# SwiGLU on one core: storing four rows per partition at once from a shared slot

## The chip, the cores and the metric

The kernel runs on 1 core of one Trainium2 chip. The metric is device time in microseconds, the median of several executions. All data is float32.

## The reference

The input `x` has 8,192 rows of 8,192 columns. Each row is split into a left half `a` and a right half `b`, and the output row (4,096 columns) is `a` times SiLU of `b`.

```python
a, b = np.split(x, 2, axis=-1)
silu_b = b / (1 + np.exp(-b))
return a * silu_b
```

So 268.44 MB are read and 134.22 MB are written, and each element is used once.

## The kernel before

A tile holds one or two neighbouring rows per partition, on 128 partitions. A row of `x` is 32 KiB, a row of the output 16 KiB. `rows` (line 26) lists the 33 tiles: one row per partition in the first and the last tile, two in the 31 between them. A two-row tile is 8.39 MB when it is loaded, and 4.19 MB when it is stored. Each partition's part is one contiguous piece of DRAM, in `x` (64 KiB) and in the output (32 KiB).

There are three SBUF slots of 64 KiB per partition, used in turn (`BUFS`, line 24). Tile i uses slot i modulo 3 for everything: `load` (line 50) fills it from the SP queue, `swiglu` (line 57) has ScalarE replace the right half by its SiLU ("gate") and VectorE multiply the halves ("product"), and the product is written over the front of the same slot; `store` (line 73) writes it out. A slot's next load waits for its store. The order is written by hand: three loads, and then for each tile the gates, the products, the store, and the load of the tile three further on. `follows_from_others` (line 40) drops those waits that follow from others, so that each instruction waits only for what comes last.

The first and the last tile are computed in two column halves (`by_halves`, line 69), tiles 1 and 31 row by row, all others in one gate (line 62) and one product (line 64).

All loads are issued by SP (line 51). Stores (line 77) are issued by ScalarE, except that the last three come from SP and two in the middle (tiles 17 and 19) from GpSimd. Each issuing engine has a DMA queue of its own, and all queues are served by the same 16 DMA engines: in the profile, q1 is SP's, q10 ScalarE's and q0 GpSimd's.

Of the kernel before, what the change touches and what calls it, by code (L numbers as in the profile page):

```python
# [1 line left out]

# [4 lines left out]

_SILU = mybir.ActivationFunctionType.Silu


@with_exitstack
def kernel(
    ctx: ExitStack,
    tc: tile.TileContext,
    x: bass.AP,
    out: bass.AP,
):

    nc = tc.nc  # L20
    N, M = x.shape
    half = M // 2
    P = nc.NUM_PARTITIONS
    BUFS = 3

    rows = [1] + [2] * (N // P // 2 - 1) + [1]
    first = [sum(rows[:i]) * P for i in range(len(rows))]
    last = len(rows) - 1

    pool = ctx.enter_context(tc.tile_pool(name="sbuf", bufs=1))  # L30
    ctx.enter_context(tc.manual_schedule())
    slots = [pool.tile([P, 2 * M], x.dtype, name=f"slot{s}") for s in range(BUFS)]
    loads, gates, prods, stores = ([[] for _ in rows] for _ in range(4))
    newest = {}

    def in_dram(t, i, width):

        return bass.AP(t.tensor, first[i] * width, [[rows[i] * width, P], [1, rows[i] * width]])

    def follows_from_others(inst, i, current, earlier):  # L40


        targets = [t for kind in current for t in kind[i]]
        targets += [t for kind in earlier for j in range(i % BUFS, i, BUFS) for t in kind[j]]
        for t in targets:
            if t is not newest.get(inst.ins.engine):
                tc.declare_no_dep(inst.ins, t.ins, reason="ordered by the other waits")
        newest[inst.ins.engine] = inst

    def load(i):  # L50
        inst = nc.sync.dma_start(  # L51
            out=slots[i % BUFS][:, : rows[i] * M], in_=in_dram(x, i, M)
        )
        follows_from_others(inst, i, [], [loads, gates, prods])
        loads[i].append(inst)

    def swiglu(i, k0, k1, c0=0, cw=half):
        view = slots[i % BUFS].rearrange("p (k s c) -> p k s c", k=2, s=2)
        a = view[:, k0:k1, 0, c0 : c0 + cw]
        b = view[:, k0:k1, 1, c0 : c0 + cw]  # L60
        o = slots[i % BUFS][:, : 2 * half].rearrange("p (k c) -> p k c", k=2)
        gate = nc.scalar.activation(out=b, in_=b, func=_SILU)  # L62
        follows_from_others(gate, i, [], [loads, gates, prods, stores])
        prod = nc.vector.tensor_mul(out=o[:, k0:k1, c0 : c0 + cw], in0=a, in1=b)  # L64
        follows_from_others(prod, i, [loads], [loads, gates, prods, stores])
        gates[i].append(gate)
        prods[i].append(prod)

    def by_halves(i):
        for c0 in range(0, half, half // 2):  # L70
            swiglu(i, 0, 1, c0, half // 2)

    def store(i):
        eng = nc.scalar if i < last - 2 else nc.sync
        if i % 2 and last // 2 <= i < last // 2 + 4:
            eng = nc.gpsimd
        inst = eng.dma_start(  # L77
            out=in_dram(out, i, half), in_=slots[i % BUFS][:, : rows[i] * half]
        )
        follows_from_others(inst, i, [loads, gates], [loads, gates, prods, stores])  # L80
        stores[i].append(inst)

    for i in range(BUFS):
        load(i)
    for i in range(last):
        if i == 0:
            by_halves(i)
        elif i in (1, last - 1):
            swiglu(i, 0, 1)
            swiglu(i, 1, 2)  # L90
        else:
            swiglu(i, 0, rows[i])
        store(i)
        if i + BUFS <= last:
            load(i + BUFS)
    by_halves(last)
    store(last)


# [1 line left out]
_INS = ['x']  # L101
_OUTS = [((8192, 4096), 'float32')]


# [23 lines left out]
```

## Time and profile before

| | |
|---|---|
| median of 3 runs | 935.07 us (934.86 to 935.34) |
| span of the profiled execution | 933.2 us |
| DMA, mean over the span | 432 GB/s, 402.67 MB |
| VectorE busy | 278.7 us (30%), 37 instructions |
| ScalarE busy | 226.8 us (24%), 38 instructions |
| product of two rows / one row / half a row | 8.69 / 4.43 / 2.29 us |
| gate of two rows / one row / half a row | 7.03 / 3.61 / 1.90 us |
| load of 8.39 MB, from issue to landing (median) | 37.7 us |
| store of 4.19 MB on ScalarE's queue, the same | 33.5 us |
| store of 4.19 MB on GpSimd's queue, the same | 34.4 us |

The profile gives the span from the first to the last instruction of one execution; it has no time of its own for that execution beyond the span, and the median of the runs is 1.87 us above it. An engine's busy time leaves out the issuing of DMAs. The time from a DMA's issue to its landing includes the time that it shares with, or waits behind, other DMAs on the same 16 engines. The trace also has a record of every DMA packet, with its size, its queue, its start and its length.

### The profile page before, as it was taken

The page shows a single profiled execution, that of the slowest core. Times are in us where ns is not written, and L with a number is a line of the kernel's source. Part 1 is how long each engine was busy: PE and PEld are TensorE (multiplying, and loading weights), DVE is VectorE, ACT ScalarE, POOL GpSimd, SP SyncE. Part 2 cuts the span into 40 slices and gives each one's busy share as a digit, 9 for nine tenths or more (in the row PEclk, how much of TensorE's full clock was granted, in tenths as well). Part 3 has the DMA queues.
Part 4 walks back from the last instruction along what each step waited for, and adds up shares of the span by engine and source line. Part 5 has one row for each costly group of instructions (what it writes and reads, how often), then busy time and mean ns, then how long its engine had stood idle before and what let it go on. Part 6 is the DMA issues. An engine that isn't in the chain of part 4 may idle for free.

```text
span 933.2 us, 220 instructions
## 1 busy us (share of the span) xinstructions
DVE 278.7 (30%) x37; ACT 226.8 (24%) x38; POOL 1.4 (0%) x6
## 2 busy tenths in 40 slices
DVE  1312333123331233312333113332133321333242
ACT  2331133311333203332033320233202332023330
POOL 0000000000000000000000000000000000000000
DMA  9999999999999999999999999999999999999998
GB/s 405 405 449 431 423 451 444 409 444 433 444 427 434 442 410 448 428 433 442 434 421 441 445 417 444 428 454 427 420 457 405 449 427 428 448 445 409 427 444 388
DMA packets 9505, 402.67 MB, mean 432 GB/s; under 512 B 1056, under 2 KB 1056, under 8 KB 1056
## 3 DMA queue, kind: packets, MB, share of 16 engines
q1 hardware_dynamic: 5184, 278.92, 69.1%
q10 hardware_dynamic: 4032, 115.35, 28.6%
q0 software_dynamic: 288, 8.39, 2.1%
q14 instruction: 1, 0.01, 0.0%
HBM read 268.44 MB, written 134.22 MB: 431 GB/s over the span
## 4 chain that ended last, share of the span: by engine, by line
DMA 72%; DVE 11%; ACT 8%; issue 6%; another core or an unknown queue 1%; DVEq 0%; POOL 0%; SPq 0%; ACTq 0%; POOLq 0%
DMA slot<-in_x_dram 40%; DMA out_dram<-slot 32%; DVE slot L64 11%; ACT slot L62 8%; DVEq L123 0%; POOL out_dram L77 0%; SPq L51 0%; ACTq L77 0%; DVEq L64 0%; POOLq L123 0%
## 5 line engine op out<-in xcount | busy, mean ns | idle before, releaser
L64 DVE TENSOR_TENSOR slot<-slot 128x8192 f32<-128x8192 f32 (+2 forms) x37 | 278.7, 7539 | 636.7 <-ACT slot L62 636.5
L62 ACT ACTIVATE slot<-slot 128x8192 f32<-128x8192 f32 (+2 forms) x37 | 225.6, 6107 | 684.3 <-DMA slot<-in_x_dram 684.3
L77 POOL DMA_DIRECT2D out_dram<-slot x2 | 1.2, 600 | 568.9 <-DVE slot L64 568.9
L62 ACT ACT_TABLE_LOAD x1 | 1.3, 1283 | 0.7 <-PEq L112 0.7
L112 POOL MEMSET const-bfloat16-1.0<- 128x1 bf16 x1 | 0.1, 102 | 0.0
L112 POOL MEMSET const-float32-0.0<- 128x1 f32 x1 | 0.1, 99 | 0.2 <-issue 0.2
L112 POOL MEMSET const-float32-1.0<- 128x1 f32 x1 | 0.1, 99 | 0.0
L112 POOL MEMSET const-uint8-127<- 128x1 uint8 x1 | 0.1, 99 | 0.0
## 6 DMA issues: line engine op xcount, KB each, us to landing
out_dram<-slot ACTq DMA_DIRECT2D x27, 4096.0 KB, 33.5
slot<-in_x_dram SPq DMA_DIRECT2D x2, 4096.0 KB, 13.6
out_dram<-slot POOLq DMA_DIRECT2D x2, 4096.0 KB, 34.4
out_dram<-slot SPq DMA_DIRECT2D x2, 4096.0 KB, 20.4
out_dram<-slot ACTq DMA_DIRECT2D x1, 2048.0 KB, 28.1
out_dram<-slot SPq DMA_DIRECT2D x1, 2048.0 KB, 16.8
slot<-in_x_dram SPq DMA_DIRECT2D x31, 37.7
```

The costliest lines, as they stand in the source:

```text
L62: gate = nc.scalar.activation(out=b, in_=b, func=_SILU)
L64: prod = nc.vector.tensor_mul(out=o[:, k0:k1, c0 : c0 + cw], in0=a, in1=b)
L77: inst = eng.dma_start(out=in_dram(out, i, half), in_=slots[i % BUFS][:, : rows[i] * half])
L112: nc = _bacc.Bacc("TRN2", target_bir_lowering=False, num_devices=1)
```

## The change

The three slots get different roles. Slot 0 is now a side slot, slots 1 and 2 are main slots. The two-row tiles are replaced: after a one-row tile (side slot) and a two-row tile (first main slot), which are stored as before, come 15 groups of four neighbouring rows per partition, and then a one-row tile. That is again 64 rows per partition.

A group is loaded in two DMAs of two rows per partition each: the first pair into a main slot, the second pair into the side slot. From one partition to the next the address in `x` now moves by four rows (128 KiB), while each piece is 64 KiB. The first pair's product goes to the front half of the main slot, in one gate and one product. The second pair is computed row by row from the side slot, and its products go to the back half of the main slot. The group is then stored in one DMA of 64 KiB per partition, 8.39 MB.

The side slot is free for the next group's second pair as soon as the group's last product is done, without a store. A main slot is loaded again after its group's store. The main slots alternate from group to group.

All loads are issued by SP, in this order: the next group's first pair (waits for the store of the group before this one), then the next group's second pair (waits for this group's last product). Stores are issued by ScalarE, those of groups 7, 8 and 9 by GpSimd, and that of group 14 and of the last row by SP. There are 33 loads as before, and 18 stores instead of 33. Waits are now named for each instruction (`after`, which drops all others).

```diff
-    BUFS = 3
-    rows = [1] + [2] * (N // P // 2 - 1) + [1]
...
+    PITCH = 4
+    groups = (N // P - 4) // 4
...
+    slots = [pool.tile([P, 2 * M], x.dtype, name=f"slot{s}") for s in range(3)]
+    side, mains = slots[0], slots[1:]
...
+    def swiglu(src, row, rows, dst, at, *needed, pieces=1):
+        view = src.rearrange("p (k s c) -> p k s c", k=2, s=2)
+        packed = dst.rearrange("p (k c) -> p k c", k=4)
+        last = None
+        for c0 in range(0, half, half // pieces):
+            cols = slice(c0, c0 + half // pieces)
+            a = view[:, row : row + rows, 0, cols]
+            b = view[:, row : row + rows, 1, cols]
+            gate = after(nc.scalar.activation(out=b, in_=b, func=_SILU), *needed)
+            last = after(
+                nc.vector.tensor_mul(out=packed[:, at : at + rows, cols], in0=a, in1=b), gate
+            )
+        return last
+
+    first = load(side, 0, 1, 1)
+    second = load(mains[0], P, 2, 2)
+    lead = [load(mains[1], 3 * P, PITCH, 2)]
+    base = 3 * P
+    firsts = {0: lead[0]}
+
+    done = swiglu(side, 0, 1, side, 0, first, pieces=2)
+    stored = store(nc.scalar, side, 0, 1, 1, done)
+    free_side = stored
+
+    def group(g):
+        return base + 4 * (g if PITCH != 4 else g * P)
+
+    seconds = {0: load(side, group(0) + 2, PITCH, 2, free_side)}
+    swiglu(mains[0], 0, 1, mains[0], 0, second)
+    done = swiglu(mains[0], 1, 1, mains[0], 1, second)
+    free = {0: store(nc.scalar, mains[0], P, 2, 2, done), 1: None}
+    last = None
+    for g in range(groups):
+        m = (g + 1) % 2
+        other = 1 - m
+        if g + 1 < groups:
+            firsts[g + 1] = load(mains[other], group(g + 1), PITCH, 2, free[other])
+        else:
+            last = load(mains[other], N - P, 1, 1, free[other])
+        swiglu(mains[m], 0, 2, mains[m], 0, firsts[g])
+        for k in range(2):
+            done = swiglu(side, k, 1, mains[m], 2 + k, seconds[g])
+        eng = nc.scalar if g + 1 < groups else nc.sync
+        if groups // 2 <= g < groups // 2 + 3:
             eng = nc.gpsimd
...
+        free[m] = store(eng, mains[m], group(g), PITCH, 4, done)
+        if g + 1 < groups:
+            seconds[g + 1] = load(side, group(g + 1) + 2, PITCH, 2, done)
+    done = swiglu(mains[1 - m], 0, 1, mains[1 - m], 0, last, pieces=2)
+    store(nc.sync, mains[1 - m], N - P, 1, 1, done)
```

In `load` and `store` the arguments after the slot are the first row, the step in rows from one partition to the next, the number of rows per partition, and what the DMA waits for.

More of the change, by code (lines that the diff above doesn't have):

```diff
@@ L23 @@
     P = nc.NUM_PARTITIONS
-    BUFS = 3
-    rows = [1] + [2] * (N // P // 2 - 1) + [1]
-    first = [sum(rows[:i]) * P for i in range(len(rows))]
-    last = len(rows) - 1
+    PITCH = 4
+    groups = (N // P - 4) // 4
     pool = ctx.enter_context(tc.tile_pool(name="sbuf", bufs=1))
     ctx.enter_context(tc.manual_schedule())
-    slots = [pool.tile([P, 2 * M], x.dtype, name=f"slot{s}") for s in range(BUFS)]
-    loads, gates, prods, stores = ([[] for _ in rows] for _ in range(4))
+    slots = [pool.tile([P, 2 * M], x.dtype, name=f"slot{s}") for s in range(3)]
@@ L34, with after @@
+    side, mains = slots[0], slots[1:]
     newest = {}
[L36 to L46, printed above, removed]
+    def after(inst, *needed):
+        for t in (t for ts in everything for t in ts):
+            if t not in needed and t is not inst and t is not newest.get(inst.ins.engine):
@@ L47, in follows_from_others, with in_dram, load @@
                 tc.declare_no_dep(inst.ins, t.ins, reason="ordered by the other waits")
         newest[inst.ins.engine] = inst
-    def load(i):
+        history.append(inst)
+        return inst
+    def in_dram(t, start, step, rows, width):
+        return bass.AP(t.tensor, start * width, [[step * width, P], [1, rows * width]])
+    history = []
+    everything = [history]
+    def load(slot, start, step, rows, *needed):
         inst = nc.sync.dma_start(
-            out=slots[i % BUFS][:, : rows[i] * M], in_=in_dram(x, i, M)
+            out=slot[:, : rows * M], in_=in_dram(x, start, step, rows, M)
@@ L53, in load @@
         )
[L54 to L75, printed above, removed]
-            eng = nc.gpsimd
[L77 to L97, printed above, removed]
+        return after(inst, *needed)
+    def store(eng, slot, start, step, rows, *needed):
+        inst = eng.dma_start(
+            out=in_dram(out, start, step, rows, half), in_=slot[:, : rows * half]
+        )
+        return after(inst, *needed)
@@ new lines, in swiglu @@
+    def swiglu(src, row, rows, dst, at, *needed, pieces=1):
[9 more added lines that the diff above has]
+                nc.vector.tensor_mul(out=packed[:, at : at + rows, cols], in0=a, in1=b), gate
+            )
+        return last
```

## The prediction

> **What bounds the kernel now.** I read the page's slices and queue table first, then windows over single stretches, then the chain of waits, then groups by form. The page shows compute engines that are mostly idle and DMA engines that are not:
>
> ```profile
> DVE 278.7 (30%) x37; ACT 226.8 (24%) x38; POOL 1.4 (0%) x6
> ...
> DMA  9999999999999999999999999999999999999998
> ...
> q1 hardware_dynamic: 5184, 278.92, 69.1%
> q10 hardware_dynamic: 4032, 115.35, 28.6%
> q0 software_dynamic: 288, 8.39, 2.1%
> ```
>
> The three queues' shares add up to 99.8% of 16 engines' span. Windows (length, busy of DVE, ACT, POOL, clock, DMA share, GB/s) say whether the mix of traffic changes the rate:
>
> ```profile
> 3.62:21.70 18.08, 4.49 (x2) 3.71 (x2) 0.00 (x0) 1.00 1.00 433
> ...
> 118.00:466.00 348.00, 104.31 (x12) 84.37 (x12) 0.00 (x0) 1.00 1.00 434
> 898.00:930.00 32.00, 13.26 (x4) 10.84 (x4) 0.00 (x0) 1.00 0.99 427
> ```
>
> The first stretch is loads alone, the second loads and stores mixed, the third stores with the one compute drain. All run at 427 to 434 GB/s. The trace's packet records give the reason: each DMA engine moves one packet after another, one of 65,536 bytes every 2.414 us, one of 32,768 bytes every 1.209 us, a completion word in 0.006 us, in every stage. A load (8.39 MB) is 8 packets per engine, 19.3 us; a store of before is 8 half packets, 9.7 us; together 8 x (2.414 + 1.209) + 0.012 = 29.00 us, and the chain's period is 29.0 us (three of its steps are 87.0). So there is no hole in the steady part. The bound is bytes, and the span can change in three ways only: the packets' sum, a hole in the queues, or the two ends. The chain shows the compute time that will matter, at a slot done as two single rows (start, length, what):
>
> ```profile
> 35.47 3.62 ACT slot L62
> ...
> 39.12 4.44 DVE slot L64
> ...
> 43.65 4.44 DVE slot L64
> 48.09 0.02 issue
> 48.11 0.34 ACTq L77
> ```
>
> The load landed at 35.44 and the store was issued at 48.11, 12.67 us later: one gate, two products, the second gate hidden behind the first product. Today another slot's load and a store fill the DMA engines meanwhile.
>
> **The change, part by part.** Names: f(g) is the load of a group's first pair into a main slot, c(g) that of the second pair into the side slot, S(g) the group's store, T the moment at which the group's last product ends.
>
> Removed and merged: 30 stores of two rows become 15 of four, in 64 KiB packets. Per engine 15 x 8 times two half packets (2.418 us) become one packet (2.414 us), 0.48 us, and 15 completion words at 0.006 go, 0.09 us. Sum -0.6 us. Loads keep number, bytes and packets.
>
> Compute: 15 two-row pairs keep their form; the other 15 become 30 + 30 single-row instructions (gate 3.61, product 4.43 us). That adds about 0.17 us of DVE per pair, hidden: f(g+1) has landed by about T + 15 and needs 15.8 us, and c(g+1) lands only at T + 45.
>
> Steady part: a group moves 25.17 MB, 58.0 us at 434 GB/s, exactly two periods of now, if the queues never run dry. c(g) ends in the engines; T comes 0.4 (from last packet to landing, by load 0) + 12.7 = 13.1 us later. Meanwhile only f(g+1) is queued, 19.3 us of it, so 6.2 us are left at T. At T S(g) is issued on ScalarE and c(g+1) on SP. The records show queues taking turns packet by packet, so the store now has half of the engines while it runs (a third before): 8 of its packets and 7 of loads, 15 x 2.414 = 36.2 us from its first packet. That first packet came 5.0 to 5.3 us after issue for the first store of the trace and 3.5 to 6.2 us for the second, both into a queue of loads alone. S(g) therefore lands 40.1 to 42.8 us after T, SP issues f(g+2) at once, and its packets start 1.0 to 1.6 us later (the first load: issue 0.74, first packets 1.74 to 2.30), at 41.1 to 44.4. The load queue runs dry at 6.2 + 19.3 + 19.3 = 44.8. The margin is 0.4 to 3.7 us, thin but positive: I take 0 here.
>
> What waits newly queue: SP's f(g+2) waits behind c(g+1), which was issued 40 us earlier; ScalarE is held by S(g)'s wait for 4.4 us behind the second gate, and what stands behind it, the gate of f(g+1), has no data until about 15 us after T. Both cost nothing.
>
> GpSimd stores: three in a row of 8.39 MB instead of two of 4.19 MB. The group of their issues has 600 ns each, and theirs took 34.4 us to land against 33.5. Started 0.3 us late and 0.9 us slower, their margin is -0.8 to 2.5 us, and a gap is bounded by one packet, 2.4 us, in up to two of three groups. I take 0 and keep +4.8 for the range.
>
> The end: this is where it pays. Before, at the last products (898 to 918) the queue still held two stores, and the last window is full. Afterwards the final one-row load (4.19 MB, 9.66 us) is all that is queued behind c(14). From c(14)'s last packet to S(14)'s first: 0.4 + 12.7 + 1.0 to 1.6 = 14.1 to 14.7 us. Covered by the load: 9.66. Hole on all 16 engines: 4.4 to 5.0 us, I take 4.8 because SP's wait and a spread of engines come on top of the low end. It doesn't depend on when the last load starts, since a late start would only move the hole ahead of it. Behind the hole, S(14) (19.3 us) hides the last row's gates and products (some 4.6 us after T), so the last store follows without a second hole.
>
> The start: three loads of the same packets, and the two early stores as before. c(0) waits for the first store as its predecessor did (47.5), f(1) for the second (81.1), while c(0) lasts until about 86. Cost 0.
>
> Sum: -0.6 + 4.8 = +4.2 us. The profiled span of 933.2 becomes 937.4; the median of the runs lies 1.87 us above that span (what lies around it), so 939.3 us. Bounds of these terms: 3.7 to 4.5, that is 938.8 to 939.6, and to 944.1 with the GpSimd gaps.
>
> A doubt is the loads' step from one partition to the next, now 128 KiB where it was 64 KiB. The trace has steps of 32 KiB (first load) and 64 KiB (the rest) at the same time per byte, 1.213 and 2.418 us a packet, so I take 0; the far end is the most stretched load packet near the start, 3.05 us instead of 2.42, which over 30 x 8 packets would be 150 us. The Trainium skill, DMA: Bandwidth & Descriptors, section Latency and other measured facts, speaks against the change here: copies fell from 214 to 207 GB/s per direction at a row pitch of 512 KiB and lower at 2 MiB, and it has no value for 128 KiB. If that first loss held here already, an estimate from that page is 3.4% of 580 us of load packets, 20 us, 959 in all.
>
> **The rivals.**
> 1. The margin fails (for: 0.4 us at its thin end, and landing waits for the slowest of 16 engines; against: both stores seen lie inside it). Every time S(g) slips by one packet, f(g+2) arrives some 2 us after the queue ran dry; the hole lengthens what is left at the next T, so every second group pays: 7 x 2 = 14 us, 953. 8%.
> 2. Only the GpSimd stage slips: 1 or 2 gaps of 2.4 us, 941.7 to 944.1. 8%.
> 3. The 128 KiB step slows load packets (for: new in this kernel; against: 32 to 64 KiB cost nothing). Each 1% on 240 packets of 2.418 us per engine costs 5.8 us; the time for 1% is 945, and nothing in the rows bounds it short of the 150 us above. 4%.
> 4. The descriptors don't go out whole: if 64 KiB stores were cut into two packets of 32 KiB, S(g) would keep a third of the engines, land after c(g+1) has ended, and leave about 1.6 us dry in each of 14 groups, 22 us: 962. Against: loads already go as 65,536-byte packets, 3,968 of them. 2%.
> 5. Not slower: a store has a cost beside its packets, and 15 fewer give it back along the steady part. It offsets the end's hole to within 0.2% from (4.2 - 1.9) / 15 = 0.15 us per store, and turns it to a gain of over 0.2% from 0.41. For: load packets near the first stores last 0.2 to 0.6 us longer. Against: 29.00 us of packets in a period of 29.0 leave under 0.05. At 0.15 to 0.4 it gives 933.3 to 937; beyond, at most 402.65 MB / 434 GB/s = 927.8 plus the ends. 6%, 2 of it on the faster side. The same page's section Anatomy of one DMA has a fixed 2.0 us per DMA; if that were exposed, 15 stores less would be worth 30 us, about 909, and the row's 434 GB/s excludes it.
>
> **How the numbers follow.** The forecast has the remaining 72%, with 938.5 to 940.5 as its own range. The range for 8 in 10 adds the GpSimd stage: 937.8 to 944.2; outside lie rivals 1, 4, 5 and most of 3, some 19%. About 0.2%, 1.9 us, is what a measurement of this kernel can tell from no change: 933.2 to 936.9 is the same. Faster 2%, same 4% (the rest of rival 5), slower 94%.
>
> **What would show it.** Right: packets of 65,536 bytes at 2.418 us on the store queue; period 58.0 us in the chain; DMA share 1.00 in windows from 100 to 890; a window near 905 to 915 with a share of about 0.5, from the last load's end to S(14)'s first packet; f(g+2) issued 1 to 4 us before c(g+1) ends. Wrong: a share under 1.00 every 116 us (rival 1), only from 530 to 720 (2), load packets over 2.418 us (3), 32,768-byte packets on the store queue (4), or no hole before the last large store.

## The result, and the profile after

The changed kernel takes 972.99 us (median of 4 runs, 970.25 to 975.44) against 935.21 us of the kernel before (4 runs, 934.86 to 936.44): a ratio of 1.0399, 95% interval 1.0386 to 1.0413. The forecast was slower, 939.3 us in a range of 937.8 to 944.2. The direction was right; the loss is 37.8 us, nine times the 4.1 us forecast. The profiled execution took 972.03 us with a span of 970.2 us, so the span grew by 37.0 us.

The page of the changed kernel, the same rows as before:

```profile
DVE 279.6 (29%) x51; ACT 228.1 (24%) x52; POOL 1.9 (0%) x7
...
DMA  9999999999999999999999999999799999999979
...
q1 hardware_dynamic: 5040, 278.92, 68.9%
q10 hardware_dynamic: 1872, 98.57, 23.5%
q0 software_dynamic: 432, 25.17, 6.0%
```

Compute is as before. The DMA row has two dents, one at about 690 us and one near the end. The queues' shares add up to 98.4%, so idle engines explain less than half of a loss of 4%. Windows of the changed kernel (length, busy of DVE, ACT and POOL, clock, DMA share, GB/s) show the rest:

```profile
207.00:218.00 11.00, 8.73 (x2) 5.74 (x2) 0.00 (x0) 1.00 0.92 399
218.00:224.00 6.00, 0.03 (x1) 0.00 (x0) 0.00 (x0) 1.00 1.05 371
224.00:262.00 38.00, 8.69 (x1) 7.03 (x1) 0.00 (x0) 1.00 1.00 433
...
408.00:466.00 58.00, 17.45 (x3) 14.15 (x3) 0.00 (x0) 1.00 0.99 414
...
684.00:690.00 6.00, 0.00 (x0) 0.51 (x1) 0.00 (x0) 1.00 0.05 22
...
940.00:945.00 5.00, 3.96 (x2) 2.22 (x2) 0.00 (x0) 1.00 0.54 229
```

Read the DMA share and the rate side by side. In one whole group (408 to 466) the engines are busy for 0.99 of the time and move 414 GB/s, not 434. From 218 to 224, right after the group's store and the next side load were issued at 218.06, the share is full and the rate is 371 GB/s: the packets themselves last longer. (Windows this short carry an error of a packet, which is why a share can exceed 1.) From 224 to 262, while the store runs, the rate is 433 GB/s. Two windows are real holes: 684 to 690, and 940 to 945 near the end.

The packet records put numbers on it. "Stretch" below is the time of packets beyond 2.418 us (64 KiB) and 1.213 us (32 KiB), summed and divided by 16 engines; "idle" is the time without a packet, per engine, from 3 us on. A "main load" fills a main slot (f in the prediction), a "side load" the side slot (c).

| us per engine | before | after | difference |
|---|---|---|---|
| stretch | 0.8 | 24.7 | +23.9 |
| idle | 0.4 | 14.2 | +13.7 |
| fewer packets and completion words (forecast's term) | | | -0.6 |
| sum | | | +37.0 |

The sum is the span's growth. The idle time is 6.0 us near 690, 4.4 us in the hole between the last load and the last large store, and 3.8 us in small pieces. The stretch sits almost wholly on load packets: of the 4,096 packets of 64 KiB on SP's queue (128 of them are the last large store's) 575 lasted over 30 ns too long, the worst 4.55 us, against 9 of the 1,792 on the two other store queues.

The chain of waits is now made of side loads and single-row compute, with a period that is not 58.0:

```profile
397.53 0.02 issue
397.54 46.89 DMA slot<-in_x_dram
444.43 0.02 issue
444.45 3.62 ACT slot L71
448.08 0.02 issue
448.10 8.77 DVE slot L73 x2
456.87 0.02 issue
456.89 49.12 DMA slot<-in_x_dram
```

From the issue of one side load (397.54) to that of the next (456.89) are 59.35 us. From landing (444.43) to issue are 12.46 us, as the prediction had it.

### The profile page after: what moved, and what is told of

It reads as the page before. It is cut to its first block, busy times and chain, and to the rows that moved or that the text cites. A ratio compares the mean times of both kernels' runs of the same rounds, so it can differ in the third digit from the quotient of the medians.

```text
span 970.2 us, 238 instructions
## 1 busy us (share of the span) xinstructions
DVE 279.6 (29%) x51; ACT 228.1 (24%) x52; POOL 1.9 (0%) x7
## 4 chain that ended last, share of the span: by engine, by line
DMA 78%; DVE 13%; ACT 6%; DVEq 0%; issue 0%
DMA slot<-in_x_dram 71%; DVE slot L73 13%; DMA out_dram<-slot 8%; ACT slot L71 6%; DVEq L138 0%
## 5 line engine op out<-in xcount | busy, mean ns | idle before, releaser
L73 DVE TENSOR_TENSOR slot<-slot 128x4096 f32<-128x4096 f32 (+2 forms) x51 | 279.6, 5511 | 669.6 <-ACT slot L71 669.5
L71 ACT ACTIVATE slot<-slot 128x4096 f32<-128x4096 f32 (+2 forms) x51 | 226.8, 4480 | 717.7 <-DMA slot<-in_x_dram 717.7
```

What stands on the lines that cost most here:

```text
L71: gate = after(nc.scalar.activation(out=b, in_=b, func=_SILU), *needed)
L73: nc.vector.tensor_mul(out=packed[:, at : at + rows, cols], in0=a, in1=b), gate
```

## The experiments

Three theories are tested below. A: loads step 128 KiB from partition to partition and collide in memory. B: loads that run alone on all 16 engines are slow at any step (in the changed kernel no store runs for about a third of each group's time). R: what counts is how late a main load is issued, by what is still queued ahead of it.

### The step of the loads (A)

Each of these three changes the third argument of the groups' loads, and the first row where needed:

```diff
-firsts[g + 1] = load(mains[other], group(g + 1), PITCH, 2, free[other])
+firsts[g + 1] = load(mains[other], group(g + 1), 2, 2, free[other])        # e1; e2: 5, e3: 8
-seconds[g + 1] = load(side, group(g + 1) + 2, PITCH, 2, done)
+seconds[g + 1] = load(side, group(g + 1) + 256, 2, 2, done)                # e1; e2: + 2, 5; e3: + 2, 8
```

> The changed kernel with the loads of the 15 groups stepping two rows (64 KiB) from one partition to the next, as in the kernel before, instead of four: a group's two loads take its first 256 rows and its second 256. Stores, waits, order and sizes stay, so the products land in other rows of the group than they belong to; the run is for its time. Theory A (the 128 KiB step makes load packets collide in memory): 64 KiB load packets fall from a mean of 2,510 to about 2,420 ns, 23 us go, 947 to 950 us, with the two holes left (6 and 5 us). Theory B (loads that run alone on all 16 engines are slower at any step): packets stay near 2,510 ns, 970 to 975 us.

> The same with a step of five rows (160 KiB), so that a group's loads read other rows than they should; the run is for its time. Theory A in the form 'a step of 128 KiB repeats over the memory's channels': an odd multiple of 32 KiB spreads again, 947 to 950 us. Theory A in the form 'any step above the piece's own 64 KiB, that is a gap between pieces, costs': 970 us or more. Theory B: 970 to 975 us.

> The same with a step of eight rows (256 KiB), rows read are not those that belong to the output; the run is for its time. Repeating channels: twice the step is worse than 128 KiB, at least 60 us of stretch instead of 24, 1,005 us or more. Theory B: 970 to 975 us. Gaps between pieces: about as with 128 KiB or somewhat more, 970 to 985 us.

The fourth gives the kernel before the 128 KiB step:

```diff
+        if rows[i] == 1 or i == 31:
+            return bass.AP(t.tensor, first[i] * width, [[rows[i] * width, P], [1, rows[i] * width]])
+        start = P + (i - 1) // 2 * 4 * P + (i - 1) % 2 * 2
+        return bass.AP(t.tensor, start * width, [[4 * width, P], [1, 2 * width]])
```

> The kernel before with its two-row tiles 1 to 30 taken in pairs from blocks of four rows per partition: loads step 128 KiB, stores 64 KiB with 32 KiB pieces. All else as before, and the output too. If the step alone slows load packets: 30 x 8 packets stretched by 92 ns each, about 22 us, 955 to 960 us. If it needs stretches in which loads run alone on all 16 engines, which this kernel hardly has: 935 to 938 us.

| run | step of loads | time, us | ratio to before | stretch, us per engine |
|---|---|---|---|---|
| changed kernel | 128 KiB | 972.99 | 1.0399 [1.0386, 1.0413] | 24.7 |
| e1 | 64 KiB | 975.78 | 1.0427 [1.034, 1.0514] | 23.9 |
| e2 | 160 KiB | 970.83 | 1.0374 [1.0337, 1.0411] | 23.7 |
| e3 | 256 KiB | 976.19 | 1.0432 [1.035, 1.0513] | 28.2 |
| e4, kernel before | 128 KiB | 935.03 | 0.9994 [0.9983, 1.0005] | 0.8 |

e1 to e3 have two runs each, and e3's profile is of its longer one (979.27 us).

Theory A falls in both directions: taking the step back to 64 KiB brings nothing, and giving it to the kernel before costs nothing. In that kernel the rate stays what it was:

```profile
118.00:466.00 348.00, 104.30 (x12) 84.35 (x12) 0.00 (x0) 1.00 1.00 434
```

### How late a load is issued (R), and the stores beside it

e5 leaves out the second side row's compute, so that everything behind the side load comes 4.4 us earlier:

```diff
-        for k in range(2):
-            done = swiglu(side, k, 1, mains[m], 2 + k, seconds[g])
+        done = swiglu(side, 0, 1, mains[m], 2, seconds[g])
```

> The changed kernel without gate and product of the second row of each side pair; its part of the output is stored as it stands. DMAs and their order stay. The last product comes 4.4 us earlier after the second load's landing, so that the next main load is issued some 7 to 9 us, not 2.8 to 4, before the load queue runs dry. Theory R (a load packet lasts longer when a load's descriptors come to a load queue that is about to run dry, and when the next DMAs come to such a queue): the stretch falls from 24 us per engine to under 4, the hole behind the GpSimd store (6 us) goes, the hole at the end falls from 4.9 to about 0.5: 936 to 942 us. Theory B (loads alone on all engines are slow; stores still fill only 38.6 of 58 us): stretch stays over 20 us, 957 to 966 us. Theory S (a 64 KiB store that comes to a queue empty of stores stretches the load packet before it): the 1.3 us at each store's issue stay, about 17 us, 951 to 957 us.

952.04 us (948.67 to 955.41), ratio 1.0182 [1.0097, 1.0267]. Stretch fell from 24.7 to 10.5 us, the hole near 690 is gone, idle is 4.4 us. The time lies in the range of S, but the stretch is neither the 4 us that R expected nor the 17 to 20 of S and B. It was not spread evenly, and that is what the run taught. Windows of e5:

```profile
100.00:420.00 320.00, 71.31 (x11) 60.26 (x11) 0.00 (x0) 1.00 1.01 435
440.00:690.00 250.00, 56.89 (x9) 45.71 (x9) 1.73 (x3) 1.00 1.00 420
```

Five groups run at full rate, with stores that still fill only two thirds of the time; then five are slow. What separates them is the load time still queued when the main load was issued (the mean of the 16 engines): 3.9 us and more in the first five, 1.9 to 3.1 in the others. Theory B can't give the first window, and S (every 64 KiB store that comes to a queue without stores costs 1.3 us) can't either. R was right in kind, and its boundary lies near 3 us.

e6 cuts each group's store in two; the output is whole:

```diff
...
+        pair = swiglu(mains[m], 0, 2, mains[m], 0, firsts[g])
+        early = store(eng, mains[m], group(g), PITCH, 2, pair)
         for k in range(2):
             done = swiglu(side, k, 1, mains[m], 2 + k, seconds[g])
-        free[m] = store(eng, mains[m], group(g), PITCH, 4, done)
+        late = store(eng, mains[m][:, 2 * half :], group(g) + 2, PITCH, 2, done)
+        free[m] = [early, late]
```

> The changed kernel with each group's store cut into two DMAs: the main pair's rows as soon as their product is done, the side pair's rows at the group's end (32 KiB pieces, 64 KiB step). The main slot is loaded again when both have landed. The late store lands some 33 us after its issue instead of 43, and a store is nearly always queued. Theories R, B and S all expect the stretch to go (under 3 us), and the end's hole to be filled by the early store: 934 to 938 us. If it stays over 15 us, none of them holds.

935.77 us (8 runs), ratio 1.0000 [0.9982, 1.0018]. Stretch 1.0, idle 0.8 us, and the window is that of the kernel before:

```profile
118.00:466.00 348.00, 104.71 (x18) 84.91 (x18) 0.00 (x0) 1.00 1.00 434
```

So the slots' new roles, the side slot and the row-by-row compute cost nothing that the runs show. The whole loss hangs on storing the group in one piece at its end. Two things changed together here: a store nearly always runs, and the main loads also come earlier, with 4.1 us of loads or more left. The next runs take them apart.

e7 and e8 make the loads of the kernel before late, by repeating a product that doesn't change the result:

```diff
+        if cw == half and k1 - k0 == 2:
+            for w in (half,):                    # e8: (half, half // 2)
+                prod = nc.vector.tensor_mul(
+                    out=o[:, 1:2, :w], in0=view[:, 1:2, 0, :w], in1=view[:, 1:2, 1, :w]
+                )
...
```

> The kernel before, with the second row's product of every whole tile made once more (4.4 us of VectorE; the output is the same). Store and next load of a slot come 4.4 us later, so a load is issued about 4 us, not 8.5, before the load queue runs dry. Stores stay 32 KiB pieces, and a store is always queued. Theory R: load packets stretch here too, some 10 to 40 us, 945 us or more. Theories B and S: nothing, 935 to 937 us (the end may take 2 us more).

> The same with 6.7 us more of VectorE for each tile: a load is issued about 1.8 us before the load queue runs dry, and comes 0.5 us or less before it does. Theory R: more stretch than in the run with 4.4 us, 955 us or more. Theories B and S: 935 to 941 us, with short holes at most.

e7: 938.93 us (938.08 to 940.88), ratio 1.0036 [1.002, 1.0052]. 28 loads, from 84 to 869 us, were issued with 0.1 to 2.4 us of loads left, later than most in the changed kernel, and none cost more than 0.05 us of stretch: beside each, packets of a store were running or began within 2.0 us (in the changed kernel, 17 us or more after the issue).

```profile
118.00:466.00 348.00, 157.40 (x24) 84.35 (x12) 0.00 (x0) 1.00 1.00 434
...
897.00:938.00 41.00, 13.34 (x4) 10.83 (x4) 0.00 (x0) 1.00 0.88 360
```

The one load that was late without a store beside it, the last at 898, cost 2.0 us of stretch and 1.2 us of idle time. R, as it stood, expected 945 or more here, and falls: lateness alone is not enough. e8: 946.82 us (943.16 to 950.48), ratio 1.0126 [1.0033, 1.0219]. The R side expected 955 or more and B and S up to 941, so it fits neither. Its 20 loads from 322 to 873 us, with 0.8 to 1.5 us left and a store's packets within 1.2 us, cost 0.1 us or less each except one (0.35). Most of its 7.9 us of stretch lie at the start, at the end, and at four loads between 117 and 275 us: one without a store, and three that came to a load queue with 0.0 to 0.5 us left and cost 0.6 to 1.4 us although a store ran.

That gives theory R2: a load costs extra where it is issued with under some 3 us of loads left in the queue **and** no store runs then. I took 91 main loads from seven kernels with 64 KiB stores (the changed one, e1 to e3, e5, and e9 and e11 below; in each the first 13 of the 14 main loads that follow a store) and sorted them by the load time left at their issue:

| loads left at issue | main loads | stretch soon after, mean, us per engine | stretch around the next store's issue, mean, us per engine | of these at least 0.7 us |
|---|---|---|---|---|
| under 3.2 us | 60 | 0.53 us | 1.23 us | 57 |
| 3.2 us and more | 31 | 0.01 us | 0.06 us | 1 |

In the records, the first part sits mostly on the late load's own first packet and, less, on its second; the second part sits mostly on the late load's last packet before the next store's first one, some 16 us later. In ten of the 12 late groups of the changed kernel's profile that packet lasts 3.5 to 3.9 us (median of the 16 engines).

The mean of 16 engines hides something. With the 14th main load of each kernel taken in, 61 of 64 under 3.2 us pay (0.7 us or more around the next store's issue), and 2 of the other 34. These two are e9's at 721 and 839 us, with a mean of 4.2 and 4.5 us left, but only 1.7 and 1.5 us on the engine that had least. The trace marks the landing of a DMA on each engine, and so this can be told of every load: sorted by the engine with least left, 63 of the 65 loads under 2.1 us pay, and none of the other 33. The limit is nearer to 2 us on the first engine to run out than to 3 us of the mean.

e9 tests R2 by taking nearly all of the side pair's compute away, with all DMAs in place:

```diff
-        for k in range(2):
-            done = swiglu(side, k, 1, mains[m], 2 + k, seconds[g])
...
+        bit = view[:, 0:1, 1, :256]
+        gate = after(nc.scalar.activation(out=bit, in_=bit, func=_SILU), seconds[g])
+        done = after(
+            nc.vector.tensor_mul(out=packed[:, 2:3, :256], in0=view[:, 0:1, 0, :256], in1=bit), gate
+        )
```

> The changed kernel with gate and product of the side pair cut to 256 columns of its first row; the rest of those two rows is stored as it stands. DMAs and their order stay, and stores still run for only two thirds of each group's time. The last product comes about 1 us after the second load's landing, so the next main load is issued with some 14 us of loads still queued. Theory R2 (a load packet is stretched where a load is issued with under some 3 us left in the load queue while no store runs, by about 0.5 us at once and 1.3 us more at that load's end): no late load, stretch 1 us as in the kernel before, no hole behind GpSimd's stores and none at the end: 934 to 936 us. Theory B (loads alone on all 16 engines are slow): stretch over 20 us, 955 us or more.

945.69 us (942.63 to 948.75), ratio 1.0107 [1.0028, 1.0187]; stretch 6.7, idle 8.8 us. The steady part is as R2 has it:

```profile
100.00:220.00 120.00, 18.23 (x4) 14.89 (x4) 0.00 (x0) 1.00 1.00 435
220.00:340.00 120.00, 18.24 (x4) 14.89 (x4) 0.00 (x0) 1.00 1.01 436
...
700.00:820.00 120.00, 18.23 (x4) 14.89 (x4) 0.00 (x0) 1.00 1.00 425
820.00:940.00 120.00, 22.73 (x6) 18.60 (x6) 0.00 (x0) 1.00 0.96 410
```

The total missed its 934 to 936. The load time left at issue shrank from group to group, from 14.0 to about 4.2 us, because a landing waits for the slowest of engines that drift apart: at 130 us the 16 engines had 13.8 to 14.4 us left, at 662 us 3.5 to 14.1. At 721 us one group paid 1.4 us and at 839 another 1.2. The end had holes that were not expected (about 7 us), and the drift is in them too: the last store landed on 12 engines by 938.5 us, on three near 942, and on one at 945.9.

e12 adds to e9 only a delay between a store's landing and the next main load, 8.7 us of VectorE on data that the load overwrites:

```diff
-            firsts[g + 1] = load(mains[other], group(g + 1), PITCH, 2, free[other])
+            needed = free[other]
+            if needed is not None:
+                for w in (2 * half,):
+                    bit = mains[other][:, :w]
+                    needed = after(nc.vector.tensor_mul(out=bit, in0=bit, in1=bit), needed)
+            firsts[g + 1] = load(mains[other], group(g + 1), PITCH, 2, needed)
```

> The kernel of e9 (side pair computed on 256 columns only) with one thing added: a multiplication of 8,192 columns on VectorE (8.7 us, in place in the free main slot, overwritten by the load) stands between a group store's landing and the issue of the next main load. The main products come behind it, so the last product moves some 3 us too. The load is then issued with 0 to 3 us of loads left where e9 had 4 to 14. Theory R2: each of 13 groups is stretched by about 0.5 us after that issue and 1.2 us at the next store's issue, as in all 57 of 60 late issues seen so far: 20 to 24 us more stretch than e9's 6, 962 to 975 us, with short holes. If the lateness is only a companion of the side pair's compute: stretch as in e9, 943 to 950 us.

981.43 us (981.27 to 981.59), ratio 1.0493 [1.0463, 1.0524], above the 962 to 975 expected, since holes came on top: idle is 21.4 us, 5.5 of them near 90 us. The stretch is what R2 said: all 13 main loads were issued with 0.0 to 0.3 us left, and each cost 0.56 to 0.74 us soon after and 1.06 to 1.32 us at the next store's issue. Total stretch is 27.0 us against 6.7 in e9, and the first windows, at 435 and 436 GB/s in e9, are slow:

```profile
100.00:220.00 120.00, 34.36 (x5) 14.89 (x4) 0.00 (x0) 1.00 0.98 411
220.00:340.00 120.00, 33.06 (x7) 14.89 (x4) 0.00 (x0) 1.00 0.98 411
```

Delaying the load's issue brings the cost back, with the same compute on the side pair, the same packets and the same steps. The multiplication that makes the delay is no rival cause, since e7 adds VectorE work in every whole tile without such a cost. But e12 tests a queue that is all but dry; for the changed kernel's own 0.8 to 2.1 us the evidence is e5 and the sorted loads.

### The hole near 690, and a repair that didn't work

e11 issues the three GpSimd stores from ScalarE:

```diff
-        if groups // 2 <= g < groups // 2 + 3:
+        if False:
```

> The changed kernel with the stores of groups 7, 8 and 9 issued by ScalarE, not by GpSimd. If the hole of 6 us after the second or third of them is due to their later landing: 963 to 969 us with 24 us of stretch left and only the end's hole. If it comes from the thin margin alone: a hole at some other group too, 970 to 975 us.

972.89 us (968.85 to 976.93), ratio 1.0398 [1.0294, 1.0502]. The holes didn't go. They moved to stores of ScalarE:

```profile
382.00:392.00 10.00, 0.00 (x0) 2.62 (x1) 0.00 (x0) 1.00 0.37 131
748.00:756.00 8.00, 0.00 (x0) 1.84 (x1) 0.00 (x0) 1.00 0.50 172
```

So GpSimd isn't the cause. A single late engine on a thin margin is: in the changed kernel, S(9) landed on 15 engines between 681.6 and 683.6 us and on the last at 689.67, when the side load queued before it had ended there too (689.47). A landing waits for the slowest engine, and the next main load came to empty queues. In e11 the last engine was 6.9 us behind the 15th at the first hole and 5.6 us at the second. Why one engine falls behind isn't shown.

e10 loads the side pair as two DMAs of one row each; the output is whole:

```diff
+    def load_rows(start, free):
+        return [load(side[:, k * M : (k + 1) * M], start + k, PITCH, 1, free[k]) for k in range(2)]
...
-        for k in range(2):
-            done = swiglu(side, k, 1, mains[m], 2 + k, seconds[g])
+        halves = [
+            swiglu(side, k, 1, mains[m], 2 + k, seconds[g][k]) for k in range(2)
+        ]
+        done = halves[1]
...
-            seconds[g + 1] = load(side, group(g + 1) + 2, PITCH, 2, done)
+            seconds[g + 1] = load_rows(group(g + 1) + 2, halves)
```

> The changed kernel with the side pair loaded as two DMAs of one row each (32 KiB pieces), the first waiting for the first side product and the second for the second; nothing else is changed and the output is the whole one. After the second landing only one gate and one product follow (8.1 us, not 12.7), and the store's 64 KiB packets meet 32 KiB load packets, so it lands some 33 us after its issue. Theory R2: the next main load is issued with 10 us or more of loads queued, stretch about 1 us, no hole behind GpSimd's stores, end hole under 1 us: 934.5 to 937 us. Theory B: as many stretches in which loads are alone, more stretch than 15 us, 950 us or more.

956.54 us (955.41 to 957.67), ratio 1.0223 [1.019, 1.0257]. No main load is late by the mean, 6.6 us or more are left at every main load (3.1 us or more on the engine with least), and up to 440 us the rate is 433 GB/s. Then it falls:

```profile
118.00:440.00 322.00, 100.30 (x17) 79.19 (x17) 0.00 (x0) 1.00 1.00 433
450.00:860.00 410.00, 118.63 (x21) 97.58 (x21) 1.73 (x3) 1.00 1.00 420
```

Its 16.7 us of stretch are of another kind: 8.2 us of them sit on store packets, which have under 0.9 us in every other kernel with 64 KiB stores. R2 doesn't cover this, and no run settled it.

## Why the prediction was wrong

**Where it held.** The bound (bytes through 16 engines at 434 GB/s, no hole in the steady part of the kernel before), the packets' saving of 0.6 us and the free moves (compute, waits of SP and ScalarE, the start) fit: e6 has all of the moves and none of the loss. The end's hole was forecast at 4.4 to 5.0 us, 4.8 taken, and measured at 4.4. (These 4.4 to 5.0 less 0.6 are 3.8 to 4.4, not the 3.7 to 4.5 that the sum gives as its bounds; that changes nothing here.) The margin was forecast at 0.4 to 3.7 us between the new load's first packets and the queue running dry; in the profile the issue comes with 0.8 to 2.1 us of loads left in most groups, less 1.0 to 1.6 us to the first packet, so near its thin end and below. The term in it that was too small is the store's time to landing: 40.1 to 42.8 us forecast, 43.2 to 45.1 measured in 12 of the first 14 groups (42.6 and 49.9 in the others). The forecast had the store's first packets 3.5 to 6.2 us after its issue; behind a late load they came after 4.8 to 8.5 us, so one late load helps to make the next one late.

**The step that failed** is the price put on that margin: "thin but positive: I take 0 here". The sum knew two states of a queue, fed or dry, and priced a dry one by its hole. The chip has a third: with one packet or so left and no store beside it, engines are idle for about 0.5 us or less per group (but for the hole near 690), while packets last longer, 0.53 us per engine at once and 1.23 us at the next store (means of the 60 late loads). The 12 late groups of the profiled run hold about 22 of its 24.7 us. The trace of before couldn't show the price: its loads had 4.4 us or more left at issue, and at all but the last a store ran or began within 2.0 us. The stretched load packets around the first store that rival 5 used, 0.2 to 0.6 us, were a hint that a packet's time can change where loads had run alone before a store came; but no load was late there, so R2 doesn't explain them.

**Rival 1** had the right place and the wrong mechanism: the loss is not a packet's slip in every second group but a stretch in nearly every one. The slip came once, at S(9), and cost 6.0 us. **Rival 2** expected gaps of 2.4 us from GpSimd's later landing; e11 shows holes like the one near 690 behind ScalarE's stores. **Rival 3** had the right symptom, longer load packets, and the wrong cause: steps of 64, 160 and 256 KiB change nothing beyond the scatter of runs, so the Trainium skill's row on pitch (DMA: Bandwidth & Descriptors, section Latency and other measured facts) plays no part up to 256 KiB; no run here shows 512 KiB. **Rival 4** fell: the store queue shows 1,408 packets of 65,536 bytes. **Rival 5** fell: 15 fewer stores gave back nothing that the packet records show beyond the 0.6 us. The fixed 2.0 us that it quotes from the Trainium skill (DMA: Bandwidth & Descriptors, section Anatomy of one DMA) is that section's figure for DMAs issued by GpSimd, and only three of the 15 large stores are.

**What stays open.** Why a late, lone load costs this much, inside the DMA engines, isn't shown; the rule is a pattern of 91 main loads and three interventions (e5, in part, and e9 took the lateness away, e12 put it back). That a store beside it removes the cost rests on e7's 28 loads and on 20 of e8's, all with stores of 32 KiB pieces (e6's main loads were not late); three other loads of e8 paid with a store beside them, so that cover isn't complete. No run puts a 64 KiB store beside a late load. e10's stretched store packets have no explanation. No version beat the kernel before: e6 and e4 equal it, within 0.2%.

## What to carry to other kernels

In a kernel bound by DMA, ask of each load how much is still queued when it is issued and whether another queue is running then; here under 3 us alone cost 1.8 us per load although engines were hardly idle. Look at the engine that runs out first, not only at the mean. Merging stores saved 0.6 us of packets, and cost 37 because it made the stores bunch: two smaller stores that keep a store queue fed and let the next load go out earlier (e6) took the whole loss back. When a profile shows a full DMA share and a lower rate, look at the length of single packets before looking for idle time.

## What was unexpected of the hardware

- A 64 KiB load packet that takes 2.418 us at any step from 64 to 256 KiB lasted 3.5 to 3.9 us (median of the engines) in ten of the 12 late groups just before a store's first packet, and over 3.0 us on 15 or all 16 engines.
- 28 loads issued with 0.1 to 2.4 us left cost 0.05 us or less each while a store ran beside them or began within 2.0 us (e7).
- In the changed kernel the first packets of a group's store started 3.8 to 6.4 us after its issue where the load before had been in time, and 4.8 to 8.5 us where it had been late: the late load's stretched packet stands before them.
- One engine of the 16 can fall 6.1 us behind the 15 others (S(9)), and a landing waits for it.
